# Attention of an encoder layer: row sums inverted once per head pair and multiplied into the loaded output, instead of into every block of probabilities

## The chip, the cores and the metric

One core of one Trainium2 chip. The metric is the device time of one execution in microseconds (us). The kernel before has a median of 1913.56 us over 3 runs (1913.49 to 1913.63). The engines are named as in the profile: PE (TensorE), DVE (VectorE), ACT (ScalarE), POOL (GpSimd, which here mainly issues DMAs) and SP (SyncE, which issues the others).

## What is computed

One layer of a bidirectional encoder in float32 with 1024 tokens and a width of 1024: a half-step feed-forward, an input projection `u @ W_in`, two attention branches, the gated merge of the two, and a second half-step feed-forward. What the change touches is the end of the softmax, in both branches:

```python
# branch A: neighbourhood attention, 8 heads of 64
p = softmax(q.k * scale + bias)
yA = p @ v
# branch B: windowed grouped attention with a sink logit, 8 heads of 64
e = exp(s - m)
p = e / (sum(e) + exp(sink - m))
yB = p @ v
h = h + (sigmoid(gA) * (yA @ W_A) + sigmoid(gB) * (yB @ W_B)) @ W_out
```

The division by the row sum is one number per query and head. It can be made on the probabilities, or later on the rows of `y`.

## The kernel before

All arithmetic is float32 made of pairs of float32r values: a matrix is split into a high part (an ACT cast, L95) and a low part (a DVE subtraction, L98), and `mm3` multiplies with three matmuls, L149, L153 and L155. The program is one long stream of PE work: first feed-forward, input projection, attention (about 915 to 1160 us in the trace), branch products and output projection, second feed-forward.

Attention runs over 64 units, each with 128 queries and two heads. Units 0 to 31 are branch B (8 blocks of queries, and for each 4 pairs of heads), units 32 to 63 branch A (4 pairs of heads `hp`, and for each 8 blocks). Step n of the loop does the scores of unit n (`scores`: two matmuls per head, L1596 and L1597, into PSUM banks of the tag "d"; the fused bias and minimum on DVE, L1601; Exp on ACT with the row sum as a second output, L1604; the reciprocal of the two sums on DVE, L1607; the first head's probabilities multiplied by it on DVE, L1608, the second's on ACT, L1609), the transposes of unit n-2 (`turn`: up to six PE transposes, L1617, into "d" banks, and their split into high and low, L95 and L98) and the product with v of unit n-3 (`values`: L1636 for B, L1631 for A, then ACT and DVE copy and add the result and SP or POOL stores it to `y_d` in DRAM: L1542 for B, L1566 for A). The tag "d" has four banks, so the transposes of one unit reuse the banks that the transposes of the unit before it left, once these have been split.

In between, `filling` gives PE other matmuls: the last gate columns of the projection (`gate`, whose results POOL stores to `g_d` at L1332), then `branch_b`, the product of `yB` with `W_B`, then the first products of branch A. Their inputs come back from DRAM. `fetch_y` (L1344 to L1346) loads 128 rows of `yB`, 512 KB, on POOL into one of four buffers with the tag "raw"; it is called four times, after the last of branch B has been stored. `split_y` (L1348 to L1355) splits such a buffer. The steps at which they are called stand in a table of the last gate column, in units of one filling step:

```python
1: lambda: [fetch_y(c * P) for c in range(2)],
2: lambda: fetch_y(2 * P),
3: lambda: split_y(Y_B[0], 0, nc.vector),
4: lambda: [split_y(Y_B[1], P, nc.vector), fetch_y(3 * P)],
6: lambda: split_y(Y_B[2], 2 * P, nc.vector)
```

For branch A `fetch_ya` (L1382) loads 128 rows of `yA` on SP, and `forms_first` makes the sums that the products need. `prep_a` (L1290) loads q, k and v of the next pair of heads; most of these loads are of 256 KB and issued by POOL (L1303, L1306). Each engine works through its own instructions in a fixed order, which a scheduler has set beforehand from the program's order and its dependences (`pin` holds some in program order). An instruction that waits holds everything behind it on its engine.

Of the kernel before, what the change touches and what calls it, by code (L numbers as in the profile page):

```python
# [15 lines left out]
P = 128  # L16
T = 1024
D = 1024
# [18 lines left out]
def trunk_kernel(ctx, tc, x, xt, n1, wg1, wu1, wd1, nm, win, rpb, sink, wa, wb, wout,  # L37
# [1131 lines left out]
    def halves(a):  # L1169
        return a[:HD], a[HD:]  # L1170
# [166 lines left out]
    def branch_mm(bs, w, y):  # L1337

        for c in range(4):
            mm3(bs, c == 0, c == 3, (w[0][:, c, :], w[1][:, c, :]),  # L1340
                [[slot(k)[:, n * 512:(n + 1) * 512] for k in y[c]] for n in range(2)])
            yield

    def fetch_y(r0):  # L1344
        mix["y", r0] = raw4()
        nc.gpsimd.dma_start(mix["y", r0], y_d[r0:r0 + P, :])  # L1346

    def split_y(slots, r0, eng):  # L1348

        h, l = [slot(k) for k in slots]  # L1350
        r = mix.pop(("y", r0))
        if r0 < 512:
            r = in_block(r)
            h, l = by_block(h), by_block(l)
        split(h, l, r, eng, True)  # L1355

    def form(k, c, src):
        h, l = [slot(i)[:, c * 512:c * 512 + 512] for i in FORMS[k]]
        split(h, l, src, None, True)
# [6 lines left out]
    def forms_first(c):  # L1366

        r = mix["ya", c]
        form("P1", c, r[:, L])
        minus(r[:, L], r[:, R], r[:, L])  # L1370
        form("P5", c, r[:, L])
# [8 lines left out]
        form(k, c, f)  # L1380

    def fetch_ya(hp):  # L1382
        r = mix["ya", hp] = raw4() if hp < 2 else new_fx(3)
        nc.sync.dma_start(r, y_d[512 + hp * P:512 + (hp + 1) * P, :])

    GROUP = dict(P1=(0, 0), P2=(0, 1), P5=(1, 0), P7=(1, 1), P6=(2, 0), P3=(2, 1), P4=(3, 0))
    bk, kept_a = {}, {}
# [143 lines left out]
    def units_b():  # L1531
        for j in range(NTT):
            for c in range(4):
                def write(o, j=j, c=c):

                    if c == 0:
                        ybox["b"] = xs4()[:HD].rearrange("p (c s t) -> p c s t", c=4, s=2)
                    lo = mix["lo"][:HD, c % 2]
                    nc.scalar.copy(lo, o[HD:])
                    nc.vector.tensor_tensor(ybox["b"][:, c], o[:HD], lo, op=ALU.add)  # L1540
                    if c == 3:
                        nc.gpsimd.dma_start(y_d[:512, j * P:(j + 1) * P].rearrange("(c s p) t -> p c s t", s=2, p=HD), ybox["b"])  # L1542

                g = c // 2
                yield dict(j=j, q=[qs_b(j)[:, 4 * s + c, :] for s in range(2)],
                           kd=[kd_b()[g]] * 2, kl=[kl_b()[g]] * 2, v=[mix["vb"][g]], bias=[mask_b] * 2,
                           sink=nsk[:, 2 * c:2 * c + 2], write=write)

    def units_a():
        for hp in range(4):  # L1550
            qs, kd, kl, va = heads_a[hp]
            for j in range(NTT):
                def write(o, j=j, hp=hp):
# [17 lines left out]
                    if j == 3:  # L1571
# [3 lines left out]
                edge = 1 if j in (0, NTT - 1) else 0  # L1575
                tj = slice(j * P, (j + 1) * P)
                yield dict(j=j, q=[qs[s][:, tj] for s in range(2)], kd=kd, kl=kl, v=va,
                           bias=[bias_at(hp, s, edge) for s in range(2)], sink=None, write=write)

    npair = [0]  # L1580

    def scores(un):
# [2 lines left out]
        nw = (k1 - k0) * P  # L1585
        moff = (k0 - j + 1) * P
        ext = 0 if un["sink"] is None else 1
        nmx, ssum, rc = small("nmx"), small("ssum"), small("rc")
# [5 lines left out]
        for s in range(2):  # L1594
# [4 lines left out]
            if ext and third:  # L1599
# [1 line left out]
            nc.vector.tensor_tensor_reduce(out=pr[:, ext:], in0=b[:, :nw], in1=un["bias"][s][:, moff:moff + nw], scale=-1.0,  # L1601
                                           scalar=un["sink"][:, s:s + 1] if ext else BIG, op0=ALU.add, op1=ALU.min,
                                           accum_out=nmx[:, s:s + 1])
            nc.scalar.activation(pr, pr, AF.Exp, scale=-1.0, bias=nmx[:, s:s + 1], accum_out=ssum[:, s:s + 1])  # L1604
            un["pr"].append(pr[:, ext:])
        npair[0] += 1
        nc.vector.reciprocal(rc, ssum)  # L1607
        nc.vector.tensor_scalar_mul(un["pr"][0], un["pr"][0], rc[:, 0:1])  # L1608
        nc.scalar.activation(un["pr"][1], un["pr"][1], AF.Copy, scale=rc[:, 1:2])  # L1609
# [45 lines left out]
    for n in range(1 << 30):  # L1655
# [25 lines left out]
        filling(n)  # L1681
        if len(pipe) > 3 and pipe[3] is not None:
# [253 lines left out]
```

## Time and profile before

| what | value |
|---|---|
| median of 3 runs | 1913.56 us (1913.49 to 1913.63) |
| profiled execution: its time | 1913.72 us |
| its span, first to last instruction | 1911.8 us |
| mean granted TensorE clock | 0.999 |
| PE busy in the span | 1902.5 us |
| attention in the trace | about 915 to 1160 us |

The trace counts from the first instruction. A row of its timeline gives the start, the duration in us, the engine, the line of the kernel, the operation, what it writes and reads, how many instructions were drawn together, and in brackets how long the engine stood idle before it and what ended that. A row of the groups gives the count after an x, then busy time, the mean duration of one in ns, and the idle time in front of such instructions with what ended it.

### The profile page before, as it was taken

The page shows a single profiled execution, that of the slowest core. Times are in us where ns is not written, and L with a number is a line of the kernel's source. Part 1 is how long each engine was busy: PE and PEld are TensorE (multiplying, and loading weights), DVE is VectorE, ACT ScalarE, POOL GpSimd, SP SyncE. Part 2 cuts the span into 40 slices and gives each one's busy share as a digit, 9 for nine tenths or more (in the row PEclk, how much of TensorE's full clock was granted, in tenths as well). Part 3 has the DMA queues.
Part 4 walks back from the last instruction along what each step waited for, and adds up shares of the span by engine and source line. Part 5 has one row for each costly group of instructions (what it writes and reads, how often), then busy time and mean ns, then how long its engine had stood idle before and what let it go on. Part 6 is the DMA issues. An engine that isn't in the chain of part 4 may idle for free.

```text
span 1911.8 us, 26094 instructions
## 1 busy us (share of the span) xinstructions
PE 1902.5 (100%) x9020; PEld 1594.4 (83%) x9020; DVE 1457.0 (76%) x2644; ACT 962.1 (50%) x1876; POOL 243.9 (13%) x453
## 2 busy tenths in 40 slices
PE   9999999999999999999999999999999999999998
PEld 8888888888888888898888888888888888888886
DVE  8988888868957788666888999789665566569664
ACT  7533545544446543444898885275333333344453
POOL 0011232210000112211112300010010001000011
PEclk9999999999999999999999999999999999999999
DMA  6256977887454367855647969653332323492341
GB/s 270 95 188 213 340 271 289 298 296 279 126 166 136 111 207 224 240 197 200 182 121 209 294 225 336 231 192 133 138 111 105 110 89 110 159 361 92 109 139 61
DMA packets 176963, 365.84 MB, mean 191 GB/s; under 512 B 17728, under 2 KB 75968, under 8 KB 176832
## 3 DMA queue, kind: packets, MB, share of 16 engines
q1 hardware_dynamic: 136784, 236.23, 37.3%
q0 software_dynamic: 39184, 126.90, 19.3%
q8 instruction: 71, 1.16, 0.3%
q10 hardware_dynamic: 864, 1.05, 0.2%
q14 instruction: 60, 0.49, 0.1%
HBM read 244.06 MB, written 121.83 MB: 191 GB/s over the span
## 4 chain that ended last, share of the span: by engine, by line
PE 97%; DVE 1%; ACT 1%; DMA 0%; issue 0%; SPq 0%; POOLq 0%; POOL 0%; DVEq 0%; ACTq 0%
PE g L149 18%; PE g L153 18%; PE g L155 18%; PE d L155 12%; PE d L149 12%; PE d L153 12%; PE d L1617 2%; PE g L1636 1%; PE d L1596 1%; PE d L1597 1%; PE g L1631 1%; PE d L142 1%; DVE ar L98 0%; DMA fx<-in_xt_dram 0%; ACT fa L1604 0%
## 5 line engine op out<-in xcount | busy, mean ns | idle before, releaser
L149 PE MATMUL g<-ar,ws 128*128 128x512 f32 x1062 | 408.3, 394 | 0.1
L153 PE MATMUL g<-ar,ws 128*128 128x512 f32 x1062 | 404.1, 390 | 0.2 <-DVE ar L98 0.2
L155 PE MATMUL g<-ar,ws 128*128 128x512 f32 x1062 | 402.7, 390 | 0.0
L149 PE MATMUL d<-ar,ws 128*128 128x512 f32 x706 | 275.2, 390 | 0.0
L153 PE MATMUL d<-ar,ws 128*128 128x512 f32 x706 | 274.9, 389 | 0.3 <-DVE ar L1000 0.3
L155 PE MATMUL d<-ar,ws 128*128 128x512 f32 x706 | 274.9, 389 | 0.1
L155 PEld LDWEIGHTS g<-ar,ws 128*128 128x128 f32 x1062 | 199.3, 188 | 42.0
L153 PEld LDWEIGHTS g<-ar,ws 128*128 128x128 f32 x1062 | 199.2, 188 | 40.8 <-DVE ar L98 0.6
L149 PEld LDWEIGHTS g<-ar,ws 128*128 128x128 f32 x1062 | 196.6, 188 | 36.7 <-ACT xs L1331 0.5
L334 DVE TENSOR_TENSOR ws<-raw,ws 128x512 fp32r<-128x512 f32 x216 | 147.6, 689 | 78.7 <-ACT ws L327 77.9
L327 ACT CAST ws<-raw 128x512 fp32r<-128x512 f32 x216 | 132.7, 620 | 143.1 <-PE g L155 60.9
L153 PEld LDWEIGHTS d<-ar,ws 128*128 128x128 f32 x706 | 132.5, 188 | 28.1 <-DVE ar L1000 0.9
L155 PEld LDWEIGHTS d<-ar,ws 128*128 128x128 f32 x706 | 132.5, 188 | 28.0 <-DVE ws L334 0.5
L149 PEld LDWEIGHTS d<-ar,ws 128*128 128x128 f32 x706 | 132.5, 188 | 27.3 <-ACT ar L998 0.2
L95 ACT CAST ws<-raw 128x512 fp32r<-128x512 f32 x88 | 54.8, 623 | 115.1 <-PE d L155 61.9
L98 DVE TENSOR_TENSOR ws<-raw,ws 128x512 fp32r<-128x512 f32 x88 | 60.5, 688 | 56.4 <-ACT ws L95 56.3
L95 ACT CAST ar<-raw 128x512 fp32r<-128x512 f32 (+1 forms) x80 | 52.2, 655 | 83.4 <-PE g L153 51.5
L446 POOL DMA_DIRECT2D hid<-fx x91 | 49.5, 544 | 343.2 <-DVE fx L506 230.5
L149 PE MATMUL g<-ws,ws 128*128 128x512 f32 x232 | 90.9, 392 | 0.0
L153 PE MATMUL g<-ws,ws 128*128 128x512 f32 x232 | 90.3, 389 | 0.0
L155 PE MATMUL g<-ws,ws 128*128 128x512 f32 x232 | 90.1, 390 | 0.0
L95 ACT CAST ws<-ar 128x512 fp32r<-128x512 f32 x104 | 64.3, 618 | 47.2 <-PE g L155 25.3
(382 smaller groups left out, 3882.5 us busy)
## 6 DMA issues: line engine op xcount, KB each, us to landing
raw<-hid SPq DMA_DIRECT2D x70, 512.0 KB
hid<-fx POOLq DMA_DIRECT2D x91, 256.0 KB, 2.8
ar<-in_ffn_w_down_dram SPq DMA_DIRECT2D x32, 512.0 KB
raw<-in_ffn_w_up_dram SPq DMA_DIRECT2D x31, 512.0 KB
wo_d<-made POOLq DMA_DIRECT2D x28, 512.0 KB, 4.4
raw<-in_ffn_w_gate_dram SPq DMA_DIRECT2D x27, 512.0 KB
hid<-fa POOLq DMA_DIRECT2D x51, 256.0 KB, 2.9
ar<-zs_d POOLq DMA_DIRECT2D x48, 256.0 KB, 8.9
```

The costliest lines, as they stand in the source:

```text
L95: hi = nc.scalar.copy(dst_hi, src)
L98: (eng or nc.vector).tensor_tensor(dst_lo, src, f32v(dst_hi), op=ALU.subtract)
L142: nc.tensor.transpose(pt[:, c * P:(c + 1) * P], xs[:, (half * 4 + c) * P:(half * 4 + c + 1) * P], ident)
L149: o = nc.tensor.matmul(b, lhs[0], r[0], start=first, stop=False, **kw)
L153: nc.tensor.matmul(b, lhs[0], r[1], start=False, stop=False, **kw)
L155: nc.tensor.matmul(b, lhs[1], r[0], start=False, stop=last, **kw)
L327: nc.scalar.copy(w[0][:, :512], a)
L334: nc.vector.tensor_tensor(w[0][:, 512:], a, f32v(w[0][:, :512]), op=ALU.subtract)
L446: nc.gpsimd.dma_start(hid[PRODUCTS.index(p), i], src)
L1596: nc.tensor.matmul(b[:, :nw], un["q"][s], un["kd"][s][:, k0 * P:k1 * P], start=True, stop=False)
L1597: nc.tensor.matmul(b[:, :nw], un["q"][s], un["kl"][s][:, k0 * P:k1 * P], start=False, stop=True)
L1617: nc.tensor.transpose(pt[:, i * P:(i + 1) * P], un["pr"][s][:, i * P:(i + 1) * P], ident)
```

## The change

Branch B and the first three pairs of heads of branch A keep their probabilities unscaled; only pair 3 of branch A (8 units) normalises as before. The row sums of the others are collected, in `sums_b` (64 columns) and `sums_a` (16 columns for each pair). At units 32, 40, 48 and 56 `inverse` takes a reciprocal of all collected sums (L1352), transposes it on PE into a "d" bank (L1354), copies it out on ACT (L1355) and stores it to `inv_d` in DRAM from POOL (L1356). When rows of `y` are loaded, `fetch_inverse` loads two rows of `inv_d` as well, each broadcast to 64 partitions (two DMAs of 256 KB in SBUF on POOL, L1360), into a "raw" buffer of their own, and `times` multiplies the two buffers on DVE (128 x 1024, L1364) ahead of the split. That happens seven times: for the four loads of `yB`, and for pairs 0, 1 and 2 of `yA`. The number of "raw" buffers stays at four. Lines of the changed kernel stand some 30 to 40 higher: `fetch_y` loads at L1368, the fused minimum is L1636, transposes L1654.

```diff
+    def inverse(t, r0):
+
+        n = t.shape[1]
+        nc.vector.reciprocal(t, t)
+        pt = bank("d")
+        nc.tensor.transpose(pt[:n, :P], t, ident)
+        nc.scalar.copy(inv_t[:n], pt[:n, :P])
+        nc.gpsimd.dma_start(inv_d[r0:r0 + n // NTT].rearrange("a (j t) -> (a j) t", t=P), inv_t[:n])
+
+    def fetch_inverse(r, r0):
+        for s, a in enumerate(halves(r)):
+            nc.gpsimd.dma_start(a, inv_d[r0 + s].partition_broadcast(HD))
+        return r
+
+    def times(a, b):
+        nc.vector.tensor_tensor(a, a, b, op=ALU.mult)
+
     def fetch_y(r0):
         mix["y", r0] = raw4()
         nc.gpsimd.dma_start(mix["y", r0], y_d[r0:r0 + P, :])
+        mix["inv", r0] = fetch_inverse(raw4(), r0 // HD)
 
     def split_y(slots, r0, eng):
 
         h, l = [slot(k) for k in slots]
         r = mix.pop(("y", r0))
+        times(r, mix.pop(("inv", r0)))
...
     def forms_first(c):
 
         r = mix["ya", c]
+        times(r, mix["inv_a", c])
...
     def fetch_ya(hp):
+        if hp == 0:
+            for c in range(2):
+                mix["inv_a", c] = raw4()
         r = mix["ya", hp] = raw4() if hp < 2 else new_fx(3)
         nc.sync.dma_start(r, y_d[512 + hp * P:512 + (hp + 1) * P, :])
+        if hp == 2:
+            mix["inv_a", 2] = fa[:, 3072:4096]
+        fetch_inverse(mix["inv_a", hp], 8 + 2 * hp)
...
-            nc.scalar.activation(pr, pr, AF.Exp, scale=-1.0, bias=nmx[:, s:s + 1], accum_out=ssum[:, s:s + 1])
+            nc.scalar.activation(pr, pr, AF.Exp, scale=-1.0, bias=nmx[:, s:s + 1], accum_out=ssum[:, s:s + 1] if sums is None else sums[s])
             un["pr"].append(pr[:, ext:])
         npair[0] += 1
+        if sums is not None:
+            return
         nc.vector.reciprocal(rc, ssum)
         nc.vector.tensor_scalar_mul(un["pr"][0], un["pr"][0], rc[:, 0:1])
         nc.scalar.activation(un["pr"][1], un["pr"][1], AF.Copy, scale=rc[:, 1:2])
...
+        if n == NTT * 4:
+            inverse(sums_b, 0)
+        elif n in (NTT * 5, NTT * 6, NTT * 7):
+            inverse(sums_a[n // NTT - 5], 2 * (n // NTT) - 2)
...
         if n == 63:
+            times(mix["ya", 2], mix["inv_a", 2])
             form("P2", 0, mix["ya", 2][:, L])
```

How the orders of two engines change at the place where the first `yB` comes back. On DVE of the kernel before, around unit 38: `hs` are the buffers of its probabilities, `d` the PSUM banks, and `ws` the split transposes of unit 36.

```order
L1601 ISA hs_7682,nmx_9478<-d_9481,fa 128x384
L1601 ISA nmx_9478 128x1
L1564 TENSOR_TENSOR fa<-g_9468,s_867_7677 64x2x128
L1601 ISA hs_7683,nmx_9478<-d_9486,fa 128x384
L1601 ISA nmx_9478 128x1
L98 TENSOR_TENSOR ws_9505<-d_9507,ws_9505 128x3x128
L1607 RECIPROCAL rc_9480<-ssum_9479 128x2
L1608 TENSOR_SCALAR hs_7682<-hs_7682,rc_9480 128x384
L98 TENSOR_TENSOR ws_9506<-d_9513,ws_9506 128x3x128
```

The same place on DVE of the kernel after; `raw_9332` holds the first 128 rows of `yB` and `raw_9334` the broadcast reciprocals.

```order
L1636 ISA hs_7682,nmx_9296<-d_9297,fa 128x384
L1636 ISA nmx_9296 128x1
L1596 TENSOR_TENSOR fa<-g_9286,s_867_7677 64x2x128
L1636 ISA hs_7683,nmx_9296<-d_9302,fa 128x384
L1636 ISA nmx_9296 128x1
L1364 TENSOR_TENSOR raw_9332<-raw_9332,raw_9334 128x1024
L98 TENSOR_TENSOR ws_9318<-d_9320,ws_9318 128x3x128
L98 TENSOR_TENSOR ws_9319<-d_9326,ws_9319 128x3x128
```

The reciprocal and the scaling are gone, and the first multiplication of `y` stands between the reductions of unit 38 and the two splits of unit 36. In the same way the second stands ahead of the reductions of unit 40, the third behind those of unit 42 (then the split of the second buffer, then the splits of unit 40), the fourth behind those of unit 44.

On POOL of the kernel before, from the last store of `yB` on (`raw` are the four loads of `fetch_y`, `ar` the loads of q and k for the next pair):

```order
L1542 DMA y_d<-xs_9177 64x8x128
L1346 DMA raw_9519<-y_d 128x1024
L1346 DMA raw_9521<-y_d 128x1024
L1332 DMA g_d<-xs_9442 128x1024
L1346 DMA raw_9570<-y_d 128x1024
L1346 DMA raw_9656<-y_d 128x1024
L1303 DMA ar_5219<-zs_d_3650 64x1024 x2
```

And of the kernel after:

```order
L1573 DMA y_d<-xs_9020 64x8x128
L1368 DMA raw_9332<-y_d 128x1024
L1360 DMA raw_9334<-inv_d 64x1024
L1332 DMA g_d<-xs_9260 128x1024
L1360 DMA raw_9334<-inv_d 64x1024
L1368 DMA raw_9337<-y_d 128x1024
L1360 DMA raw_9339<-inv_d 64x1024 x2
L1368 DMA raw_9384<-y_d 128x1024
L1303 DMA ar_5219<-zs_d_3650 64x1024 x2
L1360 DMA raw_9386<-inv_d 64x1024 x2
L1356 DMA inv_d<-s_867_7677 16x128
L1368 DMA raw_9470<-y_d 128x1024
```

The loads of reciprocals stand between those of `y`, and take "raw" buffers three and four: `raw_9384`, the third load of `yB`, now comes into a buffer that the first multiplication and split have to free, and `raw_9470`, the fourth, into one that the second has to free, with two loads of the next pair's q and k and the store of its own reciprocals in between.

More of the change, by code (lines that the diff above doesn't have):

```diff
@@ L1546, in units_b @@
                            kd=[kd_b()[g]] * 2, kl=[kl_b()[g]] * 2, v=[mix["vb"][g]], bias=[mask_b] * 2,
-                           sink=nsk[:, 2 * c:2 * c + 2], write=write)
+                           sink=nsk[:, 2 * c:2 * c + 2], write=write,
+                           sums=[sums_b[:, 16 * c + 8 * s + j:16 * c + 8 * s + j + 1] for s in range(2)])
     def units_a():
@@ L1577, in units_a @@
                 yield dict(j=j, q=[qs[s][:, tj] for s in range(2)], kd=kd, kl=kl, v=va,
-                           bias=[bias_at(hp, s, edge) for s in range(2)], sink=None, write=write)
+                           bias=[bias_at(hp, s, edge) for s in range(2)], sink=None, write=write,
+                           sums=[sums_a[hp][:, 8 * s + j:8 * s + j + 1] for s in range(2)] if hp < 3 else None)
     npair = [0]
```

8 lines of the change are left out of this document (7 added, 1 removed).

## The prediction

> **What bounds the kernel now.** First the page: busy time of each engine, and the chain that ended last, by engine.
>
> ```profile
> PE 1902.5 (100%) x9020; PEld 1594.4 (83%) x9020; DVE 1457.0 (76%) x2644; ACT 962.1 (50%) x1876; POOL 243.9 (13%) x453
> ...
> PE 97%; DVE 1%; ACT 1%; DMA 0%; issue 0%; SPq 0%; POOLq 0%; POOL 0%; DVEq 0%; ACTq 0%
> ```
>
> PE works through the whole span and is 97% of the chain. So a change pays only where PE now waits, and costs the full length of each new wait of PE. Next, stretches of the attention stage (start and end, length, then busy time of PE, weight loads, DVE, ACT and POOL, the granted clock, the busy share of the DMA engines, GB/s); the second stretch is where `yB` is fetched.
>
> ```profile
> 960.00:1008.00 48.00, 47.94 (x304) 43.35 (x303) 41.05 (x139) 43.25 (x112) 6.49 (x11) 1.00 0.40 116
> 1042.00:1060.00 18.00, 17.99 (x114) 16.05 (x113) 15.71 (x48) 14.80 (x41) 6.96 (x13) 1.00 0.97 316
> ```
>
> Even here PE works 47.94 of 48 us, while DVE (41.05) and ACT (43.25) have slack: relieving them isn't relieving PE. From 1042 us on the DMA engines are 97% busy. A PE that is held can also show as longer matmuls, so third the groups of matmuls by form in 915 to 1160 us, and the page's row of the same matmuls outside attention.
>
> ```profile
> L149 PE MATMUL g<-ar,ws 128*128 128x512 f32 x164 | 58.5, 415 | 0.1
> L153 PE MATMUL g<-ar,ws 128*128 128x512 f32 x164 | 54.7, 397 | 0.2 <-DVE ar L98 0.2
> L155 PE MATMUL g<-ar,ws 128*128 128x512 f32 x164 | 53.3, 393 | 0.0
> ```
> ```profile
> L149 PE MATMUL d<-ar,ws 128*128 128x512 f32 x706 | 275.2, 390 | 0.0
> ```
>
> Against 390 ns they lose 25, 7 and 3 ns each: 164 x 35 ns = 5.7 us. That is the ceiling of what a freer DVE and ACT can return.
>
> **What goes.** Groups of DVE, then one of ACT, from 915 to 1155 us:
>
> ```profile
> L98 DVE TENSOR_TENSOR ws<-d,ws 128x384 fp32r<-128x384 f32 x96 | 51.8, 551 | 8.0 <-ACT ws L95 7.5
> ...
> L1608 DVE TENSOR_SCALAR fa<-fa,rc 128x384 f32<-128x384 f32 x32 | 13.7, 427 | 0.6
> ...
> L1607 DVE RECIPROCAL rc<-ssum 128x2 f32<-128x2 f32 x64 | 10.5, 164 | 8.4 <-ACT fa L1604 5.0 <-ACT hs L1604 2.7
> ...
> L98 DVE TENSOR_TENSOR ar<-raw,ar 128x1024 fp32r<-128x1024 f32 x6 | 7.3, 1222 | 0.8 <-ACT ar L95 0.7
> ```
> ```profile
> L1609 ACT ACTIVATE fa<-fa,rc 128x384 f32<-128x384 f32 x32 | 19.9, 621 | 1.3 <-DVE rc L1607 1.3
> ```
>
> In 56 units DVE loses 56 x (0.164 + 0.427) = 33 us, ACT 56 x 0.621 = 35 us. On PE's path this is worth 0 to 5.7 us. I take 2.5, a little under half, because most of the loss is in L149, the matmul that follows transposes, and it is there unit after unit whatever DVE does.
>
> **What is added to the engines.** Seven multiplications of 128 x 1024, at the 1.222 us of L98 of that size 8.6 us of DVE beside PE, less than the 33 that it is given: nothing by amount. Four transposes of sums on PE: six transposes take 1050.20 - 1049.63 = 0.57 us (rows below), so four cost 0.4 us. Their reciprocals and copies, at 164 and 621 ns at most, lie in slack.
>
> **What is moved: four new waits.** This is the term that decides. DVE takes its instructions in order, and each `times` waits for three DMAs. Here are rows of before around unit 38, DVE, then PE:
>
> ```profile
> 1046.80 0.54 DVE L1601 CUSTOM_DVE_ANT_0 hs<-d,fa 128x384 f32<-128x384 f32 x1
> ...
> 1047.82 0.56 DVE L98 TENSOR_TENSOR ws<-d,ws 128x384 fp32r<-128x384 f32 x1 [0.47 <-ACT ws L95]
> ...
> 1056.26 1.23 DVE L98 TENSOR_TENSOR ar<-raw,ar 128x1024 fp32r<-128x1024 f32 x1 [0.30 <-ACT ar L95]
> ```
> ```profile
> 1049.63 0.82 PE L1617 MATMUL d<-ident,fa 128*128 128x128 f32 x6
> 1050.20 0.71 PE L149 MATMUL g<-ar,ws 128*128 128x512 f32 x2
> ...
> 1064.72 0.49 PE L1617 MATMUL d<-ident,hs 128*128 128x128 f32 x3
> ...
> 1072.71 0.49 PE L1617 MATMUL d<-ident,fa 128*128 128x128 f32 x3
> ```
>
> Before, DVE first touches `y` at 1056.26. Now the multiplication stands directly behind the reduction of 1046.80, nine microseconds earlier, and behind it wait the splits of unit 36, whose banks PE needs at 1049.63 for the transposes of unit 37. When are `y` and its reciprocals there? POOL of before:
>
> ```profile
> 1035.47 0.73 POOL L1542 DMA_DIRECT2D y_d<-xs  x1 [8.57 <-DVE xs L1540]
> 1042.24 1.14 POOL L1346 DMA_DIRECT2D raw<-y_d  x2 [6.04 <-DMA y_d<-xs]
> 1043.37 0.54 POOL L1332 DMA_DIRECT2D g_d<-xs  x1
> 1043.89 1.16 POOL L1346 DMA_DIRECT2D raw<-y_d  x2
> ...
> 1054.07 0.51 POOL L1306 DMA_DIRECT2D ar<-zs_d  x1 [1.62 <-DMA g_d<-xs]
> ...
> 1058.83 0.51 POOL L1303 DMA_DIRECT2D ar<-zs_d  x1 [2.21 <-DMA raw<-y_d]
> ...
> 1064.33 0.51 POOL L1306 DMA_DIRECT2D ar<-zs_d  x1 [0.62 <-DMA ar<-zs_d]
> ```
>
> And the times from issue to landing of the four loads of `y` (512 KB), then of the loads of q and k (256 KB) between 1000 and 1170 us:
>
> ```profile
> DMA to landing us min/median/max: 5.1/10.3/14.0
> ```
> ```profile
> DMA to landing us min/median/max: 3.3/9.6/14.8
> ```
>
> The loads can't start before 1042.24 (the last `yB` has to be in DRAM). Of what POOL then queued, the third half megabyte (`g_d`) was down at 1054.07, the fifth (the last `y`, 14.0 us after its issue at about 1044.5) at 1058.5. After the change the queue holds `y` 512, reciprocals 256, `g_d` 512, reciprocals 256 KB: 1.5 MB again, so I put the landing of the last at 1054.1.
>
> *First wait.* 1054.1, then the multiplication (1.2) and the first split of unit 36 (0.55): 1055.8 against 1049.63, so PE is held 6.1 us. If the last reciprocals are down by 1047.9 (1049.63 less those two durations), it is held 0.
>
> [...]
>
> *Second wait.* The second multiplication stands ahead of the reductions of unit 40, and behind them the new transpose of sums waits for a bank. The second pair of buffers adds 1 MB, so it is down at 1058.5 by the fifth half megabyte, when DVE, 6 us late, gets there anyway: only part of the 1.2 us of work shows. I take 0.6, between 0 and 2.
>
> *Third wait.* The third load of `y` needs a buffer, hence the first split, which ended at 1056.26 + 1.23 = 1057.5 before; 6.7 us of waits and half a multiplication later that is 1064.8. POOL then issues `y`, two loads of q and k, two of reciprocals: 1.5 MB. Lowest time to the last landing: four issues of 0.55 us ahead of it and the shortest landing of 3.3, 5.5 us; highest the 11.8 us that 1.5 MB took from 1042.24 to 1054.07. I take 8.5, near the middle, since less else is in flight then: 1073.3. Behind it DVE has the multiplication (1.2), a split of 1.2, an addition and a split of two blocks (about 0.7 together): 1076.4. PE wants the bank at 1064.72 + 6.7 = 1071.4. Held 5.0 us, 2.0 at the lowest landing, 8.3 at the highest.
>
> *Fourth wait.* The fourth load is issued when the second split is done, 1073.3 + 2.4 = 1075.7, again with 1.5 MB: 1084.2 by the same 8.5 us, and with the multiplication and one split 1085.9. PE wants that bank at 1072.71 + 6.7 + 5.0 = 1084.4: held 1.5 us, between 0 and 4.8.
>
> *Branch A's multiplications.* The tightest is the second, whose rows of `y` SP loads; in the order of after it stands behind the reductions of unit 57. Before, that load was issued, and the scores of unit 57 began, at:
>
> ```profile
> 1111.52 0.32 SPq L1384 DMA_DIRECT2D raw<-y_d  x1
> ```
> ```profile
> 1117.10 0.34 PE L1596 MATMUL d<-ar,ar 128*128 128x384 f32 x1
> ```
>
> With 5.1 us of landing it is there at 1116.6, in time; with 10.3 at 1121.8, some 3 us after the reductions would be done (about 1118.7). DVE has about 2 us in hand there: from 1047.34, the end of the reduction above, to PE's 1049.63 it is 2.3. I take 0 and keep 3 for the range.
>
> **The sum.** 6.1 + 0.6 + 5.0 + 1.5 = 13.2 us of new waits, + 0.4 of transposes, - 2.5 of relief: + 11.1. On the profiled execution of 1913.72 us that is 1924.8; the median of before lies 0.16 lower, so 1924.7, rounded to 1925. With each bound of these waits at its low end (4 for the first, if the last reciprocals overtake `g_d` and land 2 us sooner; 0; 2.0; 0) and the relief at 5.7 it is 1914; with the high ends (6.1, 2, 8.3, 4.8, and relief 0) 1935.
>
> **Rivals.** *A, the loads are in time.* This one ends on the other side, not slower. If they land as fast as the shortest rows (the last reciprocals issued three issues after 1042.24, at 1043.9, and down 3.3 us later at 1047.2, before the 1047.9 from which it decides), the first, second and fourth waits are 0 and the third is its low end of 2.0: 1913.7 + 2.0 + 0.4 - 2.5 = 1913.6, and with the whole ceiling of relief 1910.4. For it speaks that the shortest landing of a `y` (1042.24 + 5.1 = 1047.3) would be soon enough too; against it that POOL itself saw the third half megabyte down only at 1054.07. *B, POOL's queue comes too late for the third pair of branch A.* Its q and k are twelve loads, the last issued at 1064.33 before; now eight of them stand behind the fourth `y` of 1075.7 and its reciprocals, so the last is issued at 1081.5 to 1085 and lands, at 9.6 us, by 1095, at 14.8 by 1100. Its first scores stood at
>
> ```profile
> 1083.25 0.28 PE L1596 MATMUL d<-ar 128*128 128x256 f32 x1
> ```
>
> and with 13.2 us of waits come at 1096.5. So it costs nothing at the median landing, and 3 to 5 us at the highest; with the 3 us of the second multiplication of branch A that makes about 1931 (1928 to 1936).
>
> **How the numbers follow.** Forecast (PE held at the first and third loads) 0.68, A 0.2, B on top of the forecast 0.12. A difference of 0.2%, 3.8 us (1909.8 to 1917.4), is about what a measurement of this kernel tells from none. Of A a sixth (the whole ceiling and a third wait under 2.0) lies below 1909.8: faster 0.03. The rest of A, and 0.04 of the forecast's low end, lie between: same 0.21. Slower 0.76. The range is 1912 to 1935: it leaves out the lower third of A, the upper end of B and some of the forecast on either side of these bounds, in all under 0.2. The forecast by itself: 1917 to 1933.
>
> **What would show it.** Right, if in the profile after DVE stands idle in front of its first L1364, the multiplication, with a DMA of `inv_d` or `y` as what ended it, for about 6 us from 1047; if PE's transposes of unit 37 (L1654) start about 6 us late and those of unit 41 another 5; if the third `y` is issued on POOL only when the first split is done; and if L149 in the attention stage comes down from 415 ns by less than 25. Wrong, if the first L1364 starts before 1049 with no idle time, if PE's wait is named by something other than DVE, or if the L149 to L155 groups lose more than 5.7 us.

## The result, and the profile after

The change makes the kernel slower: 1930.24 us median of 6 runs (1927.64 to 1932.32), beside 1913.64 us (1913.49 to 1914.68) of the kernel before. The ratio is 1.0085, with a 95% interval of 1.0072 to 1.0098. The runs of the changed kernel spread over 4.7 us, those of before over 1.2. The profiled execution took 1929.65 us, with a span of 1927.9 and a mean clock of 0.995.

The stretches of the windows view that stand above for before (then busy PE, weight loads, DVE, ACT, POOL, granted clock, DMA share, GB/s), and three behind them:

```profile
960.00:1008.00 48.00, 48.00 (x303) 43.68 (x302) 35.44 (x113) 36.25 (x100) 6.58 (x12) 1.00 0.40 116
1042.00:1060.00 18.00, 9.51 (x53) 8.36 (x51) 7.26 (x21) 6.17 (x18) 5.39 (x10) 0.79 0.94 295
1060.00:1078.00 18.00, 17.53 (x99) 15.24 (x98) 15.51 (x37) 12.54 (x32) 8.31 (x16) 0.92 0.85 209
1078.00:1110.00 32.00, 28.40 (x168) 24.79 (x167) 24.51 (x69) 22.05 (x61) 11.12 (x19) 0.96 1.18 291
```

In 960 to 1008 DVE has lost 5.6 us of work and ACT 7.0, and PE does 303 matmuls where it did 304: relief of two engines that were not the limit. In 1042 to 1060 PE works only 9.51 of 18 us, and the granted clock, 1.00 in every such stretch of before, is 0.79 there, 0.92 in the next and 0.96 in the third. What PE waited for between 1040 and 1140 us (total, times, longest):

```profile
PE d L1654 <- DVE ws L98: 9.1, 3, 8.5
PE d L1631 <- DVE nmx L1636: 3.6, 1, 3.6
PE g L149 <- ACT xs L1331: 0.5, 1, 0.5
```

Where each begins is seen by lining up the runs by units: the start of the first scores of a unit, less its start before. The whole span of the changed kernel is 16.0 us longer, and PE's unit 63 starts 15.94 us later, so all of it is lost in attention. Two steps make it: + 11.07 from unit 39 to 40 (1049.15 and 1052.39 before, 1047.73 and 1062.04 after, hence from - 1.42 to + 9.65), and + 5.19 from unit 51 to 52 (+ 9.60 to + 14.79).

The first step on DVE, from the second reduction of unit 38 on, and on PE:

```profile
1045.07 0.54 DVE L1636 CUSTOM_DVE_ANT_0 hs<-d,fa 128x384 f32<-128x384 f32 x1
1045.54 0.08 DVE L1636 DVE_READ_ACCUMULATOR2_ANT nmx<- 128x1 f32 x1
1055.11 1.23 DVE L1364 TENSOR_TENSOR raw<-raw,raw 128x1024 f32<-128x1024 f32 x1 [9.50 <-DMA raw<-inv_d]
1056.26 1.01 DVE L98 TENSOR_TENSOR ws<-d,ws 128x384 fp32r<-128x384 f32 x2
```
```profile
1048.10 0.28 PE L1632 MATMUL d<-ar,ar 128*128 128x256 f32 x1
1056.86 1.54 PE L1654 MATMUL d<-ident,fa 128*128 128x128 f32 x6 [8.49 <-DVE ws L98]
1058.06 1.20 PE L149 MATMUL g<-ar,ws 128*128 128x512 f32 x2
```

DVE stands for 9.50 us in front of the first multiplication until a load of reciprocals lands, the splits of unit 36 wait behind it, and PE waits 8.49 us for them. Then comes what no row of before could show: the six transposes take 1.54 us instead of 0.82, and the two matmuls behind them 1.20 instead of 0.71. The windows of two microseconds show why, in the third column from the right:

```profile
1050.00:1052.00 2.00, 0.00 (x0) 0.00 (x0) 0.00 (x0) 0.00 (x0) 0.00 (x0) 1.00 1.03 414
1052.00:1054.00 2.00, 0.00 (x0) 0.00 (x0) 0.00 (x0) 0.00 (x0) 0.00 (x0) 0.64 1.05 297
...
1060.00:1062.00 2.00, 2.00 (x9) 1.81 (x8) 1.34 (x2) 0.00 (x0) 0.37 (x1) 0.50 1.18 192
1062.00:1064.00 2.00, 2.00 (x15) 1.92 (x14) 1.25 (x5) 0.93 (x3) 0.67 (x2) 0.80 1.15 216
```

The trace records two values of this clock, 1.00 and 0.50. So a value of 0.64 is 28% of the stretch at full and the rest at half clock: it fell at about 1052.6, 4.2 us after PE's last matmul, and by the 0.80 it was back at about 1062.8, 5.9 us after PE had begun again. So the step of 11.07 us is 8.49 of waiting and, by difference, 2.6 that go with the half clock. From 1052.56 to 1062.80, worked out from the 0.64 and the 0.80, is 10.24 us.

The second step, rows of POOL, SP, ACT and PE, each engine's own; first of before, the last store of gate rows, a load of another gate column and the tanh of what it brings:

```profile
1067.96 0.57 POOL L1332 DMA_DIRECT2D g_d<-xs  x1 [3.12 <-ACT xs L1331]
```
```profile
1076.62 0.32 SPq L1446 DMA_DIRECT2D xs<-g_d  x1
```
```profile
1089.39 1.08 ACT L1455 ACTIVATE xs<-xs 128x1024 f32<-128x1024 f32 x1
```

The same three after, and PE's wait:

```profile
1082.24 0.57 POOL L1332 DMA_DIRECT2D g_d<-xs  x1 [4.63 <-ACT s L1591]
```
```profile
1092.14 0.37 SPq L1477 DMA_DIRECT2D xs<-g_d  x1
```
```profile
1104.09 1.06 ACT L1486 ACTIVATE xs<-xs 128x1024 f32<-128x1024 f32 x1 [4.90 <-DMA xs<-g_d]
```
```profile
1107.71 0.69 PE L1631 MATMUL d<-ar 128*128 128x384 f32 x1 [3.60 <-DVE nmx L1636]
```

The last store of gate rows leaves late on POOL. The load doesn't read those rows (it brings an earlier column), but it comes into one of the two `xs` buffers, and in the trace it waits until this store, which reads that buffer, has landed, at 1090.00. SP issued it 2.1 us after that, because a load ahead of it in SP's order waited for PE until 1091.66. The tanh, pinned on ACT, waits for the load, ACT holds DVE and DVE holds PE: 3.60 us and again some slow clock. Before, the tanh waited for nothing.

### The profile page after: what moved, and what is told of

It is laid out like the page before. It is cut to its first block, busy times and chain, and to the rows that moved or that the text cites. A ratio compares the mean times of both kernels' runs of the same rounds, so it can differ in the third digit from the quotient of the medians.

```text
span 1927.9 us, 26104 instructions
## 1 busy us (share of the span) xinstructions
PE 1905.2 (99%) x9024; PEld 1597.0 (83%) x9024; DVE 1440.5 (75%) x2543; ACT 935.4 (49%) x1824; POOL 252.7 (13%) x471
## 4 chain that ended last, share of the span: by engine, by line
PE 95%; DMA 3%; DVE 1%; ACT 1%; issue 1%; POOL 0%; POOLq 0%; SPq 0%; ACTq 0%; DVEq 0%
PE g L149 17%; PE g L153 17%; PE g L155 17%; PE d L155 12%; PE d L149 12%; PE d L153 12%; PE d L1654 2%; DMA raw<-inv_d 1%; PE g L1673 1%; PE d L1631 1%; PE d L1632 1%; PE d L142 1%; DMA xs<-g_d 1%; PE g L1668 1%; DMA fx<-v_d 0%
## 5 line engine op out<-in xcount | busy, mean ns | idle before, releaser
L149 PE MATMUL g<-ar,ws 128*128 128x512 f32 x1062 | 407.8, 394 | 0.5 <-ACT xs L1331 0.5
L149 PE MATMUL d<-ar,ws 128*128 128x512 f32 x706 | 275.3, 390 | 0.0
L149 PEld LDWEIGHTS g<-ar,ws 128*128 128x128 f32 x1062 | 196.5, 189 | 36.9 <-ACT xs L1331 0.8
L149 PEld LDWEIGHTS d<-ar,ws 128*128 128x128 f32 x706 | 132.5, 188 | 27.2
L149 PE MATMUL g<-ws,ws 128*128 128x512 f32 x232 | 90.9, 392 | 0.0
```

The costliest lines, as they stand in the source:

```text
L149: o = nc.tensor.matmul(b, lhs[0], r[0], start=first, stop=False, **kw)
```

## The experiments

Theory W, as the prediction had it: DVE waits for the reciprocals of the first `y`, and PE behind it; to it, after the profile, come the slow clock and the late store of gate rows. The rival V: it is the work, seven multiplications and 3.5 MB of extra loads, wherever it stands. The table gives the shift of PE in us against before at the starts of six units, from the timeline of each profiled run (at unit 0 it lies between - 0.7 and + 0.5 in all), and the medians with the ratio to before. A shift is that of one execution; those of runs 1, 4, 8 and 12 took 1918.94, 1922.45, 1923.53 and 1926.43 us, more than 2 us from their medians.

| kernel | 39 | 40 | 42 | 51 | 55 | 63 | median us | ratio (95%) |
|---|---|---|---|---|---|---|---|---|
| after | -1.42 | 9.65 | 10.12 | 9.60 | 14.51 | 15.94 | 1930.24 | 1.0085 (1.0072 to 1.0098) |
| 1 relief only | -1.11 | -1.11 | -1.11 | -1.34 | 4.85 | 4.61 | 1914.61 | 1.0005 (0.9996 to 1.0014) |
| 2 no loads | 5.76 | 5.97 | 6.82 | 10.88 | 16.85 | 19.71 | 1933.77 | 1.0100 (1.0086 to 1.0114) |
| 3 loads unread | 7.84 | 8.11 | 8.22 | 8.67 | 10.67 | 16.51 | 1930.09 | 1.0087 (1.0073 to 1.0101) |
| 4 held | -1.48 | -1.48 | 5.81 | 5.69 | 6.94 | 6.96 | 1925.41 | 1.0062 (1.0047 to 1.0077) |
| 5 held, no loads | -1.65 | -1.65 | -1.65 | -0.85 | -0.84 | -1.02 | 1915.23 | 1.0009 (1.0000 to 1.0017) |
| 6 held, PE busy | -1.04 | -1.04 | 4.04 | 9.13 | 8.85 | 8.83 | 1924.83 | 1.0062 (1.0047 to 1.0077) |
| 7 held, later | -1.03 | -1.03 | -0.91 | 10.97 | 10.70 | 10.70 | 1925.87 | 1.0066 (1.0052 to 1.0079) |
| 8 as 7, gate store on SP | -0.97 | -0.97 | -0.84 | 8.19 | 7.92 | 7.93 | 1926.10 | 1.0065 (1.0051 to 1.0078) |
| 9 gate store on SP | -1.38 | 9.60 | 9.95 | 9.44 | 14.10 | 14.24 | 1927.90 | 1.0078 (1.0064 to 1.0091) |
| 10 held, early loads | -1.24 | -1.24 | 1.13 | 5.21 | 4.99 | 5.01 | 1920.37 | 1.0031 (1.0019 to 1.0043) |
| 11 branch A only | -0.14 | -0.14 | -0.02 | -0.27 | 6.22 | 13.70 | 1927.42 | 1.0076 (1.0063 to 1.0089) |
| 12 as 10, only yB held | -1.12 | -1.12 | 0.74 | 6.39 | 6.20 | 12.76 | 1923.81 | 1.0045 (1.0031 to 1.0058) |

**1. Relief only.** `times`, the calls of `inverse` and the loads of reciprocals are taken out.

```diff
 def times(a, b):
-    nc.vector.tensor_tensor(a, a, b, op=ALU.mult)
+    pass
...
-        mix["inv", r0] = fetch_inverse(raw4(), r0 // HD)
+        mix["inv", r0] = None
```

> Leaves out the whole normalisation of the seven pairs of heads (no reciprocals, no loads of them, no multiplication). Theory W (DVE waits for the first reciprocals, PE idles and its clock drops after it, later loads come late in POOL's queue): all three costs are gone and only the relief is left, 1909.5 to 1912.2 us; PE's unit 39 starts 1.4 us earlier than before, as in the changed kernel, and unit 63 by 1.4 to 4. Rival V (the work itself, multiplications and traffic, costs the time): the same here, so this run only sizes the relief for both.

Median 1914.61, in 11 runs from 1912.27 to 1921.06. That is above the 1909.5 to 1912.2 expected. In the profiled execution PE is 1.1 us ahead through unit 51, less than expected, and then loses 6.2 us between units 53 and 55, by a wait that has nothing to do with reciprocals. That execution is one of the slowest of the eleven (1918.94), so the loss is not that of a typical one. On DVE:

```profile
1102.26 0.42 DVE L1595 TENSOR_TENSOR fa<-g,s 64x256 f32<-64x256 f32 x1 [4.53 <-DMA y_d<-fa]
```

The write into the box of `yA` waits for an earlier store out of that box, and PE, 3.4 us idle, gets the slow clock as well (0.50 from 1104 to 1108). So taking 33 us of work from DVE and 35 from ACT gains nothing that the median shows (the fastest execution is 1.4 us below before): where PE comes earlier, it comes to transfers that have not become faster.

**2. Multiplications without loads.** The seven multiplications read `y` twice; no reciprocals.

```diff
-    nc.vector.tensor_tensor(a, a, b, op=ALU.mult)
+    nc.vector.tensor_tensor(a, a, a, op=ALU.max)
...
-        mix["inv", r0] = fetch_inverse(raw4(), r0 // HD)
+        mix["inv", r0] = None
```

> Keeps the seven multiplications of 128x1024, each with its own operand twice (a maximum, which leaves y as it is), without reciprocals and without their loads. Leaves out the normalisation of the seven pairs. Theory W: only y itself is waited for, the first of POOL's queue, so PE is held by at most 1.5 us at unit 37's transposes, and the time is 1910 to 1914. Rival V in the form that the multiplications cost: 7 x 1.2 us on top of the relief alone, 1918 to 1921.

1933.77 us (1929.42 to 1934.36), no faster than the changed kernel. Theory W fails in the part that named the reciprocals, and V fails as well, for 8.6 us of multiplication can't cost 20. On DVE:

```profile
1049.05 1.23 DVE L1364 TENSOR_TENSOR raw<-raw 128x1024 f32<-128x1024 f32 x1 [6.10 <-DMA raw<-y_d]
...
1124.32 1.23 DVE L1364 TENSOR_TENSOR raw<-raw 128x1024 f32<-128x1024 f32 x1 [8.05 <-DMA raw<-y_d]
```

With fewer operands to wait for, the scheduler puts the multiplications still earlier, in front of loads of `y` itself, and DVE waits 19.2 us for them, in four places.

**3. Loads unread.** As 2, but the reciprocals, their stores and 14 loads are kept, and nothing reads them.

```diff
-    nc.vector.tensor_tensor(a, a, b, op=ALU.mult)
+    nc.vector.tensor_tensor(a, a, a, op=ALU.max)
```

> As the changed kernel with all reciprocals, stores and the 14 broadcast loads, but the multiplications read y twice (a maximum) and nothing reads the loads. Leaves out the normalisation of the seven pairs. Theory W: the first multiplication waits for y alone, which lands about 1047, so the 8.5 us of idle PE at unit 37 and the slow clock after it are gone: 1914 to 1920, what is left being the late gate rows of POOL's queue (about 5 us at unit 52). Rival V in the form that 3.5 MB more traffic costs the time: 1926 to 1932, as the changed kernel.

1930.09 us, as V expected, but not by its cause: the first multiplication again waits for `y` alone, 7.31 us until 1050.06, and PE 5.9 us behind it.

```profile
1050.06 1.23 DVE L1364 TENSOR_TENSOR raw<-raw 128x1024 f32<-128x1024 f32 x1 [7.31 <-DMA raw<-y_d]
```

Against 1055.11 of the changed kernel, about 5 us of its first wait are due to the reciprocals, the rest to `y`. After 2 and 3 the theory is P: any instruction that waits for a load and that the scheduler puts ahead of the splits holds PE, whatever it loads.

**4. Held.** The change, with its multiplications kept in program order.

```diff
-    nc.vector.tensor_tensor(a, a, b, op=ALU.mult)
+    pin(nc.vector.tensor_tensor(a, a, b, op=ALU.mult))
```

> The changed kernel with the multiplications held in program order, so that the first stands some ten instructions later on DVE, behind unit 39's reductions and between the two splits of unit 37; the second a unit later too. Nothing left out. Theory W: the reciprocals land at the same 1055, DVE reaches the multiplication some 4 us later, so PE is held 4 to 6 us instead of 8.5, at unit 38's transposes instead of unit 37's: 1924 to 1928. Rival V: place does not matter, 1928 to 1932.

1925.41 us, a median 4.8 us below the changed kernel's. But its four executions fall in two pairs, 1921.99 and 1922.45, 1928.36 and 1929.53, and the second pair lies among those of the changed kernel. Why is not known; the profile is of the one of 1922.45. There PE is no longer held at unit 37, but 4.41 us at unit 38, where now the first multiplication stands between two splits. On PE:

```profile
1056.77 0.90 PE L1654 MATMUL d<-ident,hs 128*128 128x128 f32 x3 [4.41 <-DVE ws L98]
```

**5. Held, without loads.** 2 and 4 together.

```diff
-    nc.vector.tensor_tensor(a, a, b, op=ALU.mult)
+    pin(nc.vector.tensor_tensor(a, a, a, op=ALU.max))
```

> The run with multiplications and no loads of reciprocals, but with the multiplications held in program order (the first then stands behind unit 40's addition-free reductions and unit 38's splits, at about 1055 us). Leaves out the normalisation of the seven pairs. Theory P (the place: a multiplication that the scheduler put early on DVE waits for a DMA, whichever, and holds PE): with the place back where y was first touched before, PE is not held at units 37 to 41 (unit 42 starts within 1 us of before), and the time falls from 1933.8 to 1911 to 1917. Theory L (the loads of reciprocals are what is waited for) already failed; its remainder, that any multiplication behind a load costs its time, expects 1925 to 1934 as without the holding.

1915.23 us, 18.5 us less than run 2 with the same instructions in another order. No multiplication waits for a DMA, and at the six units of the table PE is 0.8 to 1.7 us ahead. The first one, on DVE, with no idle time before it:

```profile
1054.14 1.22 DVE L1364 TENSOR_TENSOR raw<-raw 128x1024 f32<-128x1024 f32 x1
```

This shows P where there are no reciprocals to load: the multiplications themselves cost next to nothing, their place costs all. With the reciprocals, place is not enough, for run 4 is 10.2 us above this one. No run holds the multiplications and loads reciprocals that nobody reads, so how much of that is traffic and how much late landing stays open; run 10, which issues some of the same loads earlier, leaves at most 5.1 us to traffic. (PE loses 1.9 us behind unit 63, where the held multiplications of `yA` come late.)

**6. Held, PE kept busy.** 4, with 20 matmuls that nobody reads in front of unit 38's transposes.

```diff
+        if n == 40:
+            b = bank("g")
+            x = u_half(0, 0)[0]
+            for i in range(20):
+                pin(nc.tensor.matmul(b, x[:, :P], x, start=True, stop=True))
```

> The changed kernel with the multiplications held in program order, and in front of unit 38's transposes 20 matmuls of 128x512 on PE whose result nobody reads (4.7 us of work put where PE was idle for 4.4 us). Nothing left out. Theory C (after such an idle stretch PE's granted clock is at half for some 5 us, which costs about 2 us more): PE starts unit 38's transposes within 0.5 us of the run without the 20 matmuls, the clock stays at 1.00, and unit 42 starts 1.5 to 2.5 us earlier, at + 3.3 to + 4.3 against before instead of + 5.8. Rival (the clock costs nothing beyond the wait): unit 42 at + 5.8 to + 6.3.

From unit 40 to 42 PE loses 5.08 us instead of the 7.29 of run 4, though it now computes through the time in which it stood idle there. Windows of run 4, then of this one:

```profile
1055.00:1057.00 2.00, 0.23 (x1) 0.23 (x2) 1.98 (x4) 0.00 (x0) 0.46 (x1) 0.63 1.10 291
1057.00:1059.00 2.00, 2.00 (x8) 1.51 (x8) 1.94 (x8) 1.20 (x4) 0.65 (x2) 0.50 1.06 250
1059.00:1061.00 2.00, 2.00 (x10) 1.90 (x9) 0.23 (x1) 1.66 (x5) 1.05 (x2) 0.50 1.33 247
```
```profile
1055.00:1057.00 2.00, 2.00 (x13) 1.65 (x11) 2.00 (x5) 0.00 (x0) 0.83 (x2) 1.00 1.06 274
1057.00:1059.00 2.00, 2.00 (x12) 1.62 (x11) 0.85 (x4) 1.63 (x6) 1.30 (x3) 1.00 1.24 255
1059.00:1061.00 2.00, 2.00 (x13) 1.65 (x12) 1.20 (x3) 1.93 (x5) 0.35 (x1) 1.00 1.22 240
```

With work of no use the clock stays at 1.00 here, and 2.2 us are saved. The whole time is that of 4 within the spread of the runs; in the trace the third and the fourth reciprocals hold DVE another 2.05 and 2.52 us.

**7. Held, and the splits of `y` two steps later.**

```diff
-                                     3: lambda: split_y(Y_B[0], 0, nc.vector),
-                                     4: lambda: [split_y(Y_B[1], P, nc.vector), fetch_y(3 * P)],
-                                     5: lambda: fetch_gate(1),
-                                     6: lambda: split_y(Y_B[2], 2 * P, nc.vector)})
+                                     4: lambda: fetch_y(3 * P),
+                                     5: lambda: [split_y(Y_B[0], 0, nc.vector), fetch_gate(1)],
+                                     6: lambda: split_y(Y_B[1], P, nc.vector),
+                                     7: lambda: split_y(Y_B[2], 2 * P, nc.vector)})
```

> The changed kernel with the multiplications held in program order and the splits of y moved two filling steps later (the first from step 3 to 5, about 5 us). Nothing left out. Theory P: the first two multiplications come after 1060, when all has landed, and PE is not held at units 37 to 41: unit 42 at - 1.4 against before. The third load of y now leaves later, because its buffer comes free only with the first multiplication, so PE is held 2 to 6 us at unit 42 or 43: 1918 to 1924 in all. Rival V (the traffic and the work cost it, not the place): 1925 or more.

1925.87 us, above what P expected. As it said, PE isn't held up to unit 42; but then DVE waits for the third reciprocals, and PE behind it for 10.0 us, where I had expected 2 to 6:

```profile
1077.97 1.23 DVE L1364 TENSOR_TENSOR raw<-raw,raw 128x1024 f32<-128x1024 f32 x1 [8.77 <-DMA raw<-inv_d]
```

The third `y` was issued at 1063.86 here, against 1056.63 in the changed kernel. It needs a buffer that the first multiplication frees, and that ended at 1061.63; the other 2.2 us are POOL's queue. Moving the first wait away starts the third load later: the four "raw" buffers tie them together. And the last of its reciprocals took 11.2 us to land, where it had taken 5.5.

**8. As 7, with the last store of gate rows on SP.**

```diff
-        nc.gpsimd.dma_start(g_d[dc * P:(dc + 1) * P, :], gt)
+        (nc.sync if dc == gates[-1] else nc.gpsimd).dma_start(g_d[dc * P:(dc + 1) * P, :], gt)
```

> The run before with the last store of gate rows issued by SP instead of POOL. Nothing left out. Theory Q (in the changed kernel the second loss, 5.2 us at unit 52, came from POOL issuing that store some 6 us late, behind the burst of loads): the tanh of the third gate column no longer waits, 2 to 5 us less than the run with the store on POOL: 1914 to 1920. If the late gate rows are of no account once the splits are moved: the same within 2 us.

1926.10 us (1923.53 to 1927.32), the same as 7. No tanh waited in 7, so there was nothing to win: of no use for the question, which 9 puts rightly.

**9. The change, with only that store on SP** (the edit of 8 alone).

> The changed kernel with only the last store of gate rows issued by SP instead of POOL. Nothing left out. Theory Q (the second loss of the changed kernel, 5.2 us at unit 52, is that store leaving 6 us late behind POOL's burst of loads, so that the tanh of the third gate column waits): unit 40 at + 9 to + 11 against before as in the changed kernel, no wait of the tanh, no step at unit 52, and 1923 to 1927. Rival (the gate rows are late because all transfers are slow there, whoever issues the store): the step stays, 1928 to 1932.

1927.90 us (1925.75 to 1933.01), which overlaps with the changed kernel's runs and misses the 1923 to 1927 of theory Q. In the trace no tanh waits for a load and the step at unit 52 is gone, as theory Q said. But PE loses 4.7 us between units 53 and 55 instead, to the wait of run 1:

```profile
1112.80 0.42 DVE L1596 TENSOR_TENSOR fa<-g,s 64x256 f32<-64x256 f32 x1 [4.29 <-DMA y_d<-fa]
```

So the store's place in POOL's queue did cause the second step, and the next transfer takes over when it is mended.

**10. Held, with early loads of the first two pairs of reciprocals.**

```diff
+        if ("inv", r0) not in mix:
             mix["inv", r0] = fetch_inverse(raw4(), r0 // HD)
...
+        if n == 34:
+            for r in (0, P):
+                mix["inv", r] = fetch_inverse(raw4(), r // HD)
```

> The changed kernel with the multiplications held in program order and the first two pairs of broadcast loads issued right behind the last store of yB, ahead of the loads of y. Nothing left out. Theory PL (place and landing: PE is held where DVE reaches a multiplication before its last operand): the first two find everything landed, so units 38 to 42 stay at - 1 to - 1.5 against before where holding alone had + 5.8; the third and fourth still wait for buffers and for loads behind other loads, 1 to 6 us: 1916 to 1922. If the loads cost by their traffic: 1923 to 1927 as with holding alone.

1920.37 us (1919.46 to 1920.59), the fastest version with the change in it, as expected. Units 38 to 42 lose 2.4 us instead of 7.3, now by `y`; a later pair of reciprocals still holds DVE 2.3 us.

```profile
1052.88 1.23 DVE L1364 TENSOR_TENSOR raw<-raw,raw 128x1024 f32<-128x1024 f32 x1 [2.17 <-DMA raw<-y_d]
...
1068.73 1.22 DVE L1364 TENSOR_TENSOR raw<-raw,raw 128x1024 f32<-128x1024 f32 x1 [2.34 <-DMA raw<-inv_d]
```

PE's wait of 2.02 us behind the first of these costs 2.4 at the next unit, with the clock at 1.00 throughout. Its wait behind the second is as long, and there the clock falls, so the length of a wait doesn't decide it alone. PE, then windows around the second wait:

```profile
1054.63 0.55 PE L1655 MATMUL d<-ident,hs 128*128 128x128 f32 x3 [2.02 <-DVE ws L98]
...
1070.81 0.69 PE L1632 MATMUL d<-ar,ar 128*128 128x384 f32 x1 [2.03 <-DVE nmx L1637]
```
```profile
1070.00:1072.00 2.00, 1.20 (x3) 1.14 (x4) 1.94 (x5) 1.98 (x4) 0.51 (x1) 0.67 1.08 250
1072.00:1074.00 2.00, 2.00 (x6) 1.57 (x5) 2.00 (x6) 0.74 (x3) 0.48 (x1) 0.50 1.19 217
```

**11. Branch A only.** Branch B normalises as before; no reciprocals or multiplications for `yB`.

```diff
-        times(r, mix.pop(("inv", r0)))
...
-        mix["inv", r0] = fetch_inverse(raw4(), r0 // HD)
...
-                           sums=[sums_b[:, 16 * c + 8 * s + j:16 * c + 8 * s + j + 1] for s in range(2)])
+                           sums=None)
```

> Branch B normalises its probabilities as before; only the first three pairs of branch A keep them unscaled, with their reciprocals through DRAM and their multiplications as in the changed kernel. Nothing left out. All theories on the loss put it into the four multiplications of yB and the loads of their reciprocals, so it goes: PE stays within 1 us of before up to unit 51, and the time is 1911.5 to 1917, what is above 1913.7 being the wait for the second load of yA. Rival (the loss comes from the 24 units of branch A, by loads that land late there): 1920 or more.

1927.42 us, a plain miss: I had put the whole loss into branch B, and branch A alone costs nearly as much as both. (Branch B alone was not run.) Up to unit 53 PE is where it was before. Then the wait for the store out of the box (5.13 us), and the second multiplication of branch A waits for its load of `y`:

```profile
1103.92 0.42 DVE L1593 TENSOR_TENSOR fa<-g,s 64x256 f32<-64x256 f32 x1 [5.13 <-DMA y_d<-fa]
...
1120.73 1.23 DVE L1364 TENSOR_TENSOR raw<-raw,raw 128x1024 f32<-128x1024 f32 x1 [5.79 <-DMA raw<-y_d]
```

On SP that load left at 1117.23, 21 us after the store that it reads, where before it was 15 us (1096.49 to 1111.52):

```profile
1096.12 0.59 SPq L1595 DMA_DIRECT2D y_d<-fa  x1
1117.23 0.32 SPq L1410 DMA_DIRECT2D raw<-y_d  x1
```

**12. As 10, but only the multiplications of `yB` held.**

```diff
-        times(r, mix.pop(("inv", r0)))
+        pin(times(r, mix.pop(("inv", r0))))
```

> As the run with held multiplications and early loads, but only the four multiplications of yB are held in program order; the three of yA stand where the scheduler puts them, as in the changed kernel. Nothing left out. Theory PL: the 1.9 us that PE loses between 1135 and 1162 us with all held comes from the held multiplications of yA and goes: 1917.5 to 1919.5, PE's lead or lag unchanged after unit 63. Rival (left free, they stand ahead of their loads as they did without loads, 8 us of DVE at unit 56): 1922 to 1930.

1923.81 us (1920.62 to 1926.43), slower than 10, so the rival holds. The loss behind unit 63 is gone (the shift stays at + 12.8 to the last matmul), but the first multiplication of `yA`, left free, waits for its reciprocals, and PE loses 6.5 us from unit 57 to 58:

```profile
1126.27 1.23 DVE L1364 TENSOR_TENSOR raw<-raw,raw 128x1024 f32<-128x1024 f32 x1 [5.05 <-DMA raw<-inv_d]
```

## Why the prediction was right, and where it was not

It said slower, 1925 us within 1912 to 1935, by PE waiting behind a multiplication that waits for a load. Direction, place and kind are right, and 2, 4 and 5 show the cause: with the place mended the median falls by 4.8 us, with the loads gone alone not at all, and with both the same work costs 1915.23. The size is not: + 11.1 us were forecast and + 16.6 measured. By its own steps:

**First wait: right, and mis-sized.** 6.1 us were predicted, 8.49 measured. The reciprocals were there a microsecond later than the 1054.1 taken from the landing of the third half megabyte (the multiplication began at 1055.11), and PE came 1.4 us earlier, through the relief. What the sum didn't have is a term for the clock: + 2.6 us after the wait, shown by the windows and by run 6. Run 4 has the same (4.41 of waiting, a step of 6.52), run 2 too (4.70 and 6.23), the first wait of run 10, of 2.0 us, has not (2.4).

**The mechanism was named too narrowly.** It said that the reciprocals decide, and that with them down by 1047.9 the wait would be 0. Runs 2 and 3 have no reciprocals to wait for, and still hold PE 4.7 and 5.9 us, for `y` itself lands at 1049 to 1050, not at 1047.3. Rival A, for which the landing as fast as the shortest row was the condition, did not come about: first in POOL's queue, `y` took 6.0 us to 1049.05 in run 2 and 7.3 us to 1050.06 in run 3.

**Second wait: small, as said.** Unit 40 to 41 adds 0.45 us.

**Third and fourth wait: wrong.** 5.0 and 1.5 us were predicted, and neither multiplication waited for long: of 11.0 us that DVE waited for reciprocals in all, 9.5 are the first, and from unit 42 to 45 PE gains 0.75 us. The step that failed is "The third load of `y` needs a buffer, hence the first split". POOL after:

```profile
1056.63 0.57 POOL L1368 DMA_DIRECT2D raw<-y_d  x1 [10.80 <-DVE raw L1364]
...
1061.63 1.03 POOL L1360 DMA_DIRECT2D raw<-inv_d  x2 [3.37 <-DVE raw L1364]
```

It was released by the multiplication, not the split, which ran only from 1066.19 to 1067.41: the buffer of the reciprocals is free as soon as they have been read, so the load left at 1056.63 and not at 1064.8, and the last of its reciprocals landed at 1067.61, before DVE came to them at 1070.87. The fourth load needed the first split and not the second: it left at 1068.35. So two of the signs that the prediction named, the later transposes of unit 41 and the third load behind the first split, didn't appear; DVE's and PE's first wait did. Where the first multiplication comes late, as in 7, the same wait does appear, with 8.77 us.

**Rival B: the right kind, another victim.** It put POOL's lateness on q and k of the third pair and on the second multiplication of branch A. In the changed kernel neither held PE by more than a microsecond; the store of gate rows did, by 5.19 us from unit 51 to 52. So its 1931 (1928 to 1936) fits the measured time by luck, and that the forecast's range holds it is in part luck too: 6.5 us of waits that did not come stand against 2.6 of clock and 5.2 of gate rows that were not foreseen, 2.4 more of the first wait and 1.1 less of relief.

**Relief: - 1.42 us by unit 39** (and nothing later that can be told), where 2.5 were put. Runs 1 and 5 have 1.1 to 1.65 at that unit. The L149 rows did not come down: from 915 to 1040 us they have 413 ns after and 414 before, so most of the 5.7 us called a ceiling was not to be had.

**Transposes and multiplications** (0.4 us and nothing): run 5 bears out the second; the first is too small to see.

Why does the store of gate rows leave late? It stood ready when ACT had copied its second half, at 1076.2, and left at 1082.24; POOL had issued eight loads in a burst from 1073.39 on, and in this program POOL's DMAs take eight semaphores in turn (111 to 118 in both traces). Of the 395 in the trace that have another eight places ahead, none left before that one had landed, and of the 377 of before none either. For the store that is the load of 1073.39, of which it needs nothing. In the trace it landed 8.3 us later, at 1081.69, POOL's wait on its semaphore ended at 1081.72, and the store left at 1082.24. (The row names ACT, for a copy that began at 1081.59, but the copies that the store needs had ended by 1076.2.) Rows of before in the prediction are of the same kind: the load of 1054.07, which reads `zs_d`, waits for the landing of a store into `g_d`, eight places ahead. Open is why the store out of `yA`'s box takes 15 us in one kernel and 21 in another.

## What to carry to other kernels

Work that was taken off engines with slack bought nothing here, while one instruction that waits for a transfer, put on the in-order queue of an engine that feeds the bound engine, can cost nearly its whole wait (9.50 us of DVE's became 8.49 of PE's): look for each new one at where the scheduler put it, what stands behind it, and when its last operand lands. Before such a change, list the transfers that land just in time; this kernel had at least four between 1042 and 1125 us (the first `y`, the gate rows, the store out of `yA`'s box, the loads of `yA`), and each took over when the one before it was mended. And price what comes on top of a long PE wait: waits of 4.4, 4.7 and 8.5 us cost 2.1, 1.5 and 2.6 us more in this kernel.

## What the runs showed of the hardware that was not expected

How long PE waits is not all that decides the granted clock: in run 10 a wait of 2.02 us left it at 1.00, and with one of 2.03 us it fell to 0.50. Of the thirteen profiled executions with the change or a part of it, twelve have a mean clock of 0.995 to 0.998; run 5 has 0.999, as before. Where windows show both ends of a stretch at half clock, its length, worked out as above, is 10.24 and 3.41 us in the changed kernel (from 1052.56 and from 1107.18), 6.84 in run 1 (from 1102.48), 3.42 in run 2 (from 1050.18), 6.84 in run 4 (from 1055.52) and 6.84 in run 11 (from 1120.56): one, two or three times 3.41, as far as the two digits of a window tell. The stretch at full clock between the two of the changed kernel, 44.38 us, is 13 times as long. The fall came 1.9 (run 10) to 4.2 us (the changed kernel) after a wait of PE had begun, and in these six stretches the return 2.8 (run 2) to 6.1 us (run 1) after it had ended. Why the clock fell with one of two waits of the same length, and not with the other, was not shown.

A loss of 2.2 us could be had back by matmuls of no use, in run 6: the one place where more work on the bound engine made a step shorter.
